# Stores of a dilated convolution: one hardware queue, or a software queue for six of eight pairs

## The chip, the cores and the metric

The kernel runs on one core of one Trainium2 chip. Its time is the device time of one execution in microseconds (us), from three runs. A profile of one further execution shows what each engine did: PE is TensorE (matmuls), DVE VectorE, ACT ScalarE, POOL GpSimd, and SP SyncE, which here only issues transfers. Sixteen DMA engines move the data between the chip's main memory and the core's on-chip memory.

## The reference

A 3x3 convolution with dilation 2 and padding 2 over 16 images of 64 channels, 64 x 64 pixels, to 128 channels, all in float32:

```python
x_pad = np.pad(x, ((0, 0), (0, 0), (pad, pad), (pad, pad)), mode='constant')   # pad = 2
for b in range(batch):            # 16
    for co in range(c_out):       # 128
        for ci in range(c_in):    # 64
            for kh in range(k):   # 3
                for kw in range(k):
                    output[b, co] += weight[co, ci, kh, kw] * x_pad[b, ci, kh*dilation:kh*dilation+h, kw*dilation:kw*dilation+w]
```

The input is 16.8 MB and the output 33.6 MB, so two thirds of the traffic are stores.

## The kernel before, in words

Two images form a pair: their 2 x 64 channels fill the 128 partitions, and there are eight pairs. A pair is loaded as one float32 tile of 2 MB (`load`, L65; pair 0 in two pieces), into a ring of three (`XF`). Each pair is worked in four groups of 16 rows, so there are 32 groups G. For a group, `cast` turns the float32 rows into float16 (L83 on ACT, L85 on POOL for four early groups), `rowsum` adds neighbouring pairs of rows on DVE (L95), and `product` runs the matmuls (L186) into three PSUM tiles: psP from the row sums, psA for the even and psB for the odd blocks of rows. ACT copies psP to `p_sb` (L248), and DVE adds it to psA and to psB (L254) and writes the finished rows to the output ring `o_ring`. That ring holds three pairs (`OB`), two images of 2 MB each: the place of pair p is written again by pair p + 3, so its stores must have ended by then.

The order of all instructions is written out by hand (a manual schedule): every engine runs its own in program order. The table `CASTS` says in which group a cast stands: from pair 3 on, a cast stands eight groups (for the last two pairs six) ahead of the group that uses it, in ACT's order just behind the copy of p_sb. A cast that waits for its load therefore holds up ACT, and with it the p_sb copies of later groups. The table `LOADS` says after which group a load is issued: pair 3 after group 0, 4 after 2, 5 after 3, 6 after 7, 7 after 11; it waits until the casts have emptied its place in the ring.

All transfers are issued by SP into its queue, in this order: weights, pairs 0 to 2, pair 3, a small store of the first four rows of the first image (`store(0, 0, 0, GR // 4)`, 128 KB), pairs 4 and 5, the two images of pair 0 (`pair_store`), those of pair 1, the load of pair 6, the stores of pair 2, the load of pair 7, and then the stores pair by pair. The flag `later` puts the stores of pairs 1 and 2 ahead of the load that stands in the same group. The last pair is stored by halves; one piece of its second image goes as 124 and 4 partitions. A store waits on SP until DVE has written its rows, and what follows it on SP waits too.

Of the kernel before, what the change touches and what calls it, by code (L numbers as in the profile page):

```python
# [10 lines left out]
def kernel(  # L11
# [7 lines left out]
    nc = tc.nc  # L19
# [16 lines left out]
    GR = 16  # L36
    NG = H // GR
    NBLK = GR // 4
    NH = GR // 2 * W
    npairs = B // 2  # L40
# [21 lines left out]
    def load(pb, cuts=(0, H)):  # L62
        x32_tiles[pb] = fpool.tile([P, HW], f32, tag="x32", name="x32")
        for lo, hi in zip(cuts[:-1], cuts[1:]):
            nc.sync.dma_start(  # L65
                out=x32_tiles[pb][:, lo * W : hi * W], in_=x_pair[pb, :, lo * W : hi * W]
            )
# [3 lines left out]
    def o_pair(pb):  # L71
        at = pb % OB * 2 * HW
        return o_ring[:, at : at + 2 * HW]
# [13 lines left out]
    def rowsum(c):  # L87
        pb, g = divmod(c, NG)
        if g == 0:
            xs_tiles[pb] = sxpool.tile([P, HW // 2], f16, tag="xs", name="xs")  # L90
        v = x16_tiles[pb][:, g * GR * W : (g + 1) * GR * W].rearrange(
            "p (b e q) -> p b e q", e=2, q=2 * W
        )
        s = xs_tiles[pb][:, g * NH : (g + 1) * NH].rearrange("p (b q) -> p b q", q=2 * W)
        nc.vector.tensor_tensor(out=s, in0=v[:, :, 0], in1=v[:, :, 1], op=add)  # L95
# [76 lines left out]
    def casts(G):  # L172
        for c, eng in CASTS.get(G, ()):
            cast(c, eng)

    def product(ps, src, kind, blk0, nblk, first, last):
        for j in (1, 0, 2):
            dw = (j - 1) * d
            o0, o1 = max(0, -dw), W - max(0, dw)
            t = kind * KW + j  # L180
            for hb in range(2):
                pp = slice(hb * CI, (hb + 1) * CI)
                rhs = src(pp, dw + o0, dw + o1)
                po = ps[:, hb * NH + blk0 * 2 * W : hb * NH + (blk0 + nblk) * 2 * W]
                po = po.rearrange("p (r w) -> p r w", w=W)[:, :, o0:o1]
                nc.tensor.matmul(  # L186
                    out=po,
                    lhsT=w_sb[pp, t * CO : (t + 1) * CO],
                    rhs=rhs,
                    start=first and j == 1,  # L190
                    stop=last and j == 2,
                )

    def blocks(x16, b0, n, e):
        v = x16.rearrange("p (b e r w) -> p b e r w", e=2, r=2, w=W)
        return lambda pp, c0, c1: v[pp, b0 : b0 + n, e, :, c0:c1]

    def store(pb, m, r0=0, r1=H, rows=((0, P),)):
        for lo, hi in rows:
            nc.sync.dma_start(  # L200
                out=out_img[2 * pb + m, lo:hi, r0 * W : r1 * W],
                in_=o_pair(pb)[lo:hi, m * HW + r0 * W : m * HW + r1 * W],
            )

    def pair_store(pb):
        for m in range(2):
            store(pb, m, GR // 4 if pb == m == 0 else 0)

    LOADS = {0: (3,), 2: (4,), 3: (5,), 7: (6,), 11: (7,)}
    FOUR = ((0, P - 4), (P - 4, P))  # L210
# [2 lines left out]
    for G in range(ngroups):  # L213
        pb, g = divmod(G, NG)
        x16 = x16_tiles[pb]
        xs = xs_tiles[pb].rearrange("p (r w) -> p r w", w=W)
        o = o_pair(pb).rearrange("p (m b e q) -> p m b e q", m=2, e=2, q=2 * W)
        b0 = g * NBLK

        def summed():  # L220
            ps = ppool.tile([P, 2 * NH], f32, tag="p", name="psP")
            sv = lambda pp, c0, c1: xs[pp, g * GR // 2 : (g + 1) * GR // 2, c0:c1]
            product(ps, sv, 0, 0, NBLK, True, True)
            return ps

        def even():
            ps = apool.tile([P, 2 * NH], f32, tag="ab", name="psA")
            product(ps, blocks(x16, b0, NBLK, 1), 1, 0, NBLK, True, False)
            z = 1 if g == 0 else 0
            product(ps, blocks(x16, b0 + z - 1, NBLK - z, 1), 2, z, NBLK - z, False, True)  # L230
            return ps

        def odd():
            ps = apool.tile([P, 2 * NH], f32, tag="ab", name="psB")
            product(ps, blocks(x16, b0, NBLK, 0), 3, 0, NBLK, True, False)
            z = 1 if g == NG - 1 else 0
            product(ps, blocks(x16, b0 + 1, NBLK - z, 0), 4, 0, NBLK - z, False, True)
            return ps

        if G == 0:  # L240
            psA, psP, psB = even(), summed(), odd()
        else:
            psP, psA, psB = summed(), even(), odd()

        if not G:
            casts(-1)
        p_sb = spool.tile([P, 2 * NH], f32, tag="psb", name="p_sb")
        nc.scalar.copy(out=p_sb, in_=psP)  # L248
        casts(G)
        if G + 1 < ngroups:  # L250
            rowsum(G + 1)
        pv = p_sb.rearrange("p (m b q) -> p m b q", m=2, q=2 * W)
        for e, ps in ((0, psA), (1, psB)):
            nc.vector.tensor_tensor(  # L254
                out=o[:, :, b0 : b0 + NBLK, e],
                in0=ps.rearrange("p (m b q) -> p m b q", m=2, q=2 * W),
                in1=pv,
                op=add,
            )

        later = pb in (1, 2)
        if g == NG - 1 and later:
            pair_store(pb)
        for q in LOADS.get(G, ()):
            load(q)
        if G == 0:
            store(0, 0, 0, GR // 4)
        if pb == npairs - 1:
            if g % 2 == 1:
                store(pb, 0, (g - 1) * GR, (g + 1) * GR)  # L270
                if g == 1:
                    store(pb, 1, 0, 2 * GR - ROWS4)
                    store(pb, 1, 2 * GR - ROWS4, 2 * GR, FOUR)
                else:
                    store(pb, 1, (g - 1) * GR, (g + 1) * GR)
        elif g == NG - 1 and not later:
            pair_store(pb)


# [33 lines left out]
```

## Time and profile before

| What | Value |
|---|---|
| Time of three runs | 126.86 us median (126.48 to 128.02) |
| Time of the profiled execution | 126.87 us |
| Its span, first to last instruction | 125.1 us |
| Busy share of PE, DVE, ACT, POOL | 84%, 72%, 49%, 5% |
| Data in SP's queue (q1) | 50.63 MB, 96.6% of the sixteen DMA engines' time |
| Read and written | 17.07 MB and 33.55 MB |
| Stores of a whole image | 13 of 2048 KB, 20.6 us (median) from issue to landing |

The page of the profile gives, for each engine, its busy time and share, then the span in 40 slices with a digit for each engine (9 is 90% busy or more), the DMA engines' busy share and the data rate in GB/s. Groups and waits are listed by source line (L254 is line 254 of the kernel). A table of stretches gives the same quantities for any times that one asks for; a list in order of time gives start, duration, engine, line, operation, and in brackets how long the engine was idle before it and what ended that wait. SPq stands for SP's issuing of transfers, not for the transfers.

### The profile page before, as it was taken

How to read it: one execution, taken by the hardware profiler on the slowest of the kernel's cores; microseconds unless marked ns; L12 is line 12 of the kernel's file. 1: busy time of each engine (PE TensorE's matmuls, PEld its weight loads, DVE VectorE, ACT ScalarE, POOL GpSimd, SP SyncE). 2: the span in 40 equal slices, each digit the busy share in tenths (PEclk: the TensorE clock that was granted, in tenths of full speed). 3: DMA queues.
4: the chain of work that ended last, by engine and by line, in shares of the span. 5: the costliest groups of instructions: out<-in, count | busy, mean ns of one | idle time of the engine just before them, and what ended most of it. 6: DMA issues, size and time to landing. Idle time of an engine off the chain costs nothing.

```text
span 125.1 us, 2341 instructions
## 1 busy us (share of the span) xinstructions
PE 105.5 (84%) x1000; PEld 56.6 (45%) x1000; DVE 90.4 (72%) x103; ACT 61.2 (49%) x64; POOL 6.1 (5%) x12
## 2 busy tenths in 40 slices
PE   6999999989999999999999999999999999300000
PEld 2355555535555555555555555555555555100000
DVE  0566969859998889888988898888988887700000
ACT  4279597396666666666336665666533333000000
POOL 2402306000000000000000000000000000000000
PEclk9999999999999999999999999999999999995555
DMA  4999999999999999999999999999999999999991
GB/s 136 376 447 440 440 419 424 419 440 419 287 419 436 424 430 440 411 424 445 424 422 430 424 419 445 430 424 424 435 430 414 435 440 424 424 419 411 430 390 63
DMA packets 4322, 50.78 MB, mean 406 GB/s; under 512 B 472, under 2 KB 600, under 8 KB 1112
## 3 DMA queue, kind: packets, MB, share of 16 engines
q1 hardware_dynamic: 4312, 50.63, 96.6%
q8 instruction: 8, 0.13, 0.4%
q14 instruction: 2, 0.02, 0.0%
HBM read 17.07 MB, written 33.55 MB: 405 GB/s over the span
## 4 chain that ended last, share of the span: by engine, by line
PE 64%; DVE 1%; DVEq 1%; issue 0%
PE psA L186 26%; PE psB L186 25%; PE psP L186 13%; DVE osb L254 1%; DVEq L308 1%; DVEq L254 0%
## 5 line engine op out<-in xcount | busy, mean ns | idle before, releaser
L186 PEld LDWEIGHTS <-w_sb 64*128 64x128 f16 x960 | 54.3, 94 | 45.6 <-issue 1.0
L248 ACT COPY p_sb<-psP 128x1024 f32<-128x1024 f32 x32 | 32.4, 1011 | 36.1 <-issue 18.6
L254 DVE TENSOR_TENSOR osb<-psA,p_sb 128x1024 f32<-128x1024 f32 x32 | 39.2, 1224 | 13.4 <-PE psA L186 7.6
L186 PE MATMUL psA<-x,w_sb 64*128 64x496 f16 (+3 forms) x384 | 45.1, 365 | 0.1
L186 PE MATMUL psB<-x,w_sb 64*128 64x496 f16 (+3 forms) x384 | 45.1, 365 | 0.0
L254 DVE TENSOR_TENSOR osb<-psB,p_sb 128x1024 f32<-128x1024 f32 x32 | 39.0, 1220 | 0.0
L83 ACT CAST x<-x 128x1024 f16<-128x1024 f32 (+2 forms) x27 | 28.2, 1051 | 4.4 <-DMA x<-in_x_dram 4.4
L186 PE MATMUL psP<-xs,w_sb 64*128 64x496 f16 (+1 forms) x192 | 26.0, 372 | 0.5 <-ACT p_sb L248 0.5
L95 DVE TENSOR_TENSOR xs<-x 128x512 f16<-128x512 f16 x32 | 13.3, 416 | 0.5 <-ACT x L83 0.5
L111 PE MATMUL dm<-zero 128*128 128x512 f16 x10 | 4.6, 580 | 1.2 <-DVE zero L103 1.2
L85 POOL CAST x<-x 128x896 f16<-128x896 f32 (+1 forms) x4 | 3.9, 987 | 12.5 <-DMA x<-in_x_dram 12.5
L111 PEld LDWEIGHTS <-zero 128*128 128x128 f16 x10 | 1.1, 124 | 2.7 <-issue 1.4
L121 DVE CAST wd<-w 128x192 f16<-128x192 f32 x1 | 0.5, 505 | 2.4 <-DMA w<-in_weight_dram 2.4
L134 PEld LDWEIGHTS <-wd 128*64 128x64 f16 x30 | 1.3, 140 | 2.1 <-DVE wd L121 1.1
L134 PE MATMUL wt<-ident,wd 128*64 128x128 f16 x30 | 1.9, 278 | 0.2 <-DVE wd L121 0.2
L123 ACT ACT_TABLE_LOAD x1 | 1.3, 1283 | 0.7 <-PEq L294 0.7
L146 ACT CAST w_sb<-wt 128x384 f16<-128x384 f32 x1 | 0.5, 478 | 2.0 <-PE wt L134 2.0
L148 DVE CAST w_sb<-wt 128x384 f16<-128x384 f32 x1 | 0.6, 558 | 1.2 <-PE wt L134 1.2
L123 ACT CAST wd<-w 128x192 f16<-128x192 f32 x1 | 0.5, 538 | 1.5 <-DMA w<-in_weight_dram 1.5
L122 POOL TENSOR_TENSOR wd<-w 128x192 f16<-128x192 f32 x1 | 0.8, 796 | 2.3 <-DMA w<-in_weight_dram 2.3
L103 DVE MEMSET zero<- 128x256 uint32 x1 | 0.3, 272 | 0.9 <-PEq L294 0.9
L125 POOL CAST wd<-w 128x192 f16<-128x192 f32 x1 | 0.8, 800 | 0.0
(12 smaller groups left out, 4.4 us busy)
## 6 DMA issues: line engine op xcount, KB each, us to landing
out_dram<-osb SPq DMA_DIRECT2D x13, 2048.0 KB, 20.6
x<-in_x_dram SPq DMA_DIRECT2D x7, 2048.0 KB, 14.8
out_dram<-osb SPq DMA_DIRECT2D x3, 1024.0 KB, 14.9
out_dram<-osb SPq DMA_DIRECT2D x1, 1920.0 KB, 19.0
x<-in_x_dram SPq DMA_DIRECT2D x1, 1088.0 KB, 5.5
x<-in_x_dram SPq DMA_DIRECT2D x1, 960.0 KB, 7.4
out_dram<-osb SPq DMA_DIRECT2D x1, 768.0 KB, 16.4
w<-in_weight_dram SPq DMA_DIRECT2D x1, 288.0 KB, 2.8
```

What stands on the lines that cost most here:

```text
L83: eng.copy(out=out, in_=in_)
L85: eng.tensor_copy(out=out, in_=in_)
L95: nc.vector.tensor_tensor(out=s, in0=v[:, :, 0], in1=v[:, :, 1], op=add)
L111: nc.tensor.matmul(out=dm[:, 0:512], lhsT=zero[:, 0:P], rhs=zero)
L122: nc.gpsimd.tensor_tensor(out=wdv[:, 3], in0=wv[:, 0], in1=wv[:, 1], op=sub)
L123: nc.scalar.copy(out=wdv[:, 2], in_=wv[:, 0])
L125: nc.gpsimd.tensor_copy(out=wdv[:, 4], in_=wv[:, 2])
L134: nc.tensor.matmul(out=wts[k % 3][r * CI : (r + 1) * CI, c0 + j * CO : c0 + (j + 1) * CO], lhsT=wd[:, t * CI : (t + 1) * CI], rhs=ident,)
L186: nc.tensor.matmul(out=po, lhsT=w_sb[pp, t * CO : (t + 1) * CO], rhs=rhs, start=first and j == 1, stop=last and j == 2,)
L248: nc.scalar.copy(out=p_sb, in_=psP)
L254: nc.vector.tensor_tensor(out=o[:, :, b0 : b0 + NBLK, e], in0=ps.rearrange("p (m b q) -> p m b q", m=2, q=2 * W), in1=pv, op=add,)
L308: with _tile.TileContext(nc) as tc:
```

## The change

The stores of pairs 0 to 5 are issued from GpSimd, through its software queue, in place of SP; those of pairs 6 and 7 stay on SP. The early store of four rows is gone, and the first image of pair 0 is stored whole. The flag `later` is gone as well: in a group with both, the load now stands ahead of the pair's stores in the program. Loads stay on SP, in the same groups. The stores on GpSimd stand in its program order behind its casts of groups 0 to 3, and it has no other work after these.

```diff
+    SOFT = range(npairs - 2)
+
     def store(pb, m, r0=0, r1=H, rows=((0, P),)):
+        queue = nc.gpsimd if pb in SOFT else nc.sync
         for lo, hi in rows:
-            nc.sync.dma_start(
+            queue.dma_start(
                 out=out_img[2 * pb + m, lo:hi, r0 * W : r1 * W],
                 in_=o_pair(pb)[lo:hi, m * HW + r0 * W : m * HW + r1 * W],
             )
 
     def pair_store(pb):
         for m in range(2):
-            store(pb, m, GR // 4 if pb == m == 0 else 0)
+            store(pb, m)
...
-        later = pb in (1, 2)
-        if g == NG - 1 and later:
-            pair_store(pb)
         for q in LOADS.get(G, ()):
             load(q)
-        if G == 0:
-            store(0, 0, 0, GR // 4)
         if pb == npairs - 1:
...
-        elif g == NG - 1 and not later:
+        elif g == NG - 1:
             pair_store(pb)
```

## The prediction

> **What bounds the kernel now.** I read the page from the top, then the stretches, then the waits of single instructions.
>
> ```profile
> PE 105.5 (84%) x1000; PEld 56.6 (45%) x1000; DVE 90.4 (72%) x103; ACT 61.2 (49%) x64; POOL 6.1 (5%) x12
> DMA  4999999999999999999999999999999999999991
> q1 hardware_dynamic: 4312, 50.63, 96.6%
> out_dram<-osb SPq DMA_DIRECT2D x13, 2048.0 KB, 20.6
> ```
>
> PE is the busiest engine, but the DMA engines are full in every slice but the first and the last, and all data goes through one queue, SP's (q1). A 2 MB store lands 20.6 us after its issue though it needs only 4.9 us: the rest is queue ahead of it.
>
> ```profile
> 30.00:33.00 3.00, 3.00 (x33) 1.69 (x30) 2.91 (x4) 1.85 (x2) 0.00 (x0) 1.00 1.00 306
> 33.00:36.00 3.00, 3.00 (x34) 1.71 (x31) 2.83 (x4) 2.06 (x2) 0.00 (x0) 1.00 0.95 389
> 36.00:60.00 24.00, 24.00 (x238) 13.17 (x234) 21.19 (x25) 14.61 (x16) 0.00 (x0) 1.00 1.01 430
> 60.00:108.00 48.00, 47.45 (x460) 25.81 (x456) 42.13 (x46) 22.73 (x23) 0.00 (x0) 1.00 1.01 428
> 108.00:120.00 12.00, 0.00 (x0) 0.00 (x0) 0.80 (x1) 0.00 (x0) 0.00 (x0) 0.67 1.00 419
> 120.00:123.00 3.00, 0.00 (x0) 0.00 (x0) 0.00 (x0) 0.00 (x0) 0.00 (x0) 0.50 0.71 298
> ```
>
> The last columns are the DMA engines' busy share and GB/s. The rate is 428 to 430 in the long stretches, also in 36 to 60 us, where loads stand among stores. It dips once, in 30 to 36 us (1.1 us lost). After 108.8 us nothing computes and some 14 us of stores are still draining. So **bytes at 428 GB/s set the end**: a 2 MB image (2.097 MB) is 4.9 us, and the change can lose time wherever DMA runs dry or slows, and gain only what DMA wastes now.
>
> ```profile
> 24.75 1.15 ACT L83 CAST x<-x 128x1152 f16<-128x1152 f32 x1 [2.19 <-DMA x<-in_x_dram]
> 34.85 1.16 ACT L83 CAST x<-x 128x1152 f16<-128x1152 f32 x1
> 59.81 1.23 DVE L254 TENSOR_TENSOR osb<-psA,p_sb 128x1024 f32<-128x1024 f32 x1 [0.15 <-ACT p_sb L248]
> 84.98 1.22 DVE L254 TENSOR_TENSOR osb<-psA,p_sb 128x1024 f32<-128x1024 f32 x1 [0.58 <-DMA out_dram<-osb]
> ...
> 22.11 13.53 SPq L200 DMA_DIRECT2D out_dram<-osb  x4
> 35.74 0.60 SPq L65 DMA_DIRECT2D x<-in_x_dram  x1
> ```
>
> These fix the order of the queue. Call the load of pair p Lp and its two stores Sp. L3 has landed at 24.7. Then come L4, L5, S0, S1, L6, S2, L7, S3: 12 images, 58.8 us, less 0.3 for the piece of S0 that went early, plus the dip: S3 lands at 84.3. The trace has DVE waiting for S3 (its place in the ring of three output pairs) until 84.98. So the hand schedule holds within 0.7 us, and I use it for the change.
>
> **The change, part by part.** The profiled execution took 126.87 us, the median of the three times is 126.86; its span is 125.1, so 1.8 us lie around the span. I sum against 126.87.
>
> *Issues.* Twelve 2 MB stores leave SP for POOL, and the 128 KB store of four rows goes into its image. SP's issues took 0.33 to 0.70 us each; POOL's store issue has no row. POOL's last other work is its casts, ending at 21.51 us, ahead of the first store in its order, so no compute queues behind a store; even 1 to 2 us each (a POOL cast is 1.0, nearest row of that engine) is 12 to 24 us on an engine that is empty for 100. From issue to first byte I take 2 us (the 288 KB weight load on SP landed in 2.8 whole); bounds 0.3 and 10, because L4 and L5 keep DMA fed to 34.5 us. Sum 0; without that backlog it is the full 2 us per store.
>
> *SP's waits.* SP no longer stands 75.6 us in L200 for DVE. L6 was issued at 35.74, behind S1; now it follows its cast (31.84 + 0.94 = 32.8), and L7 likewise 45.2 instead of 48.06. Neither load starts earlier for that, as others are ahead of it. Sum 0.
>
> *Order.* This is the main part: stores now meet loads on the DMA engines instead of standing behind them. No row shows two data queues at once. Bounds: all turns to loads gives the old order, 0; all turns to stores is the first rival, +9. I take equal turns, as both queues then hold 16 KB rows. From 24.2 us (store issue at 22.1 plus 2) each gets half: an image takes 9.8 us.
> - L4 24.7 to 34.5 us; ACT's cast wants it at 34.85. It just fits, 0 to 1 us late.
> - L5 lands at 44.3 (cast wants it at 47.2), L6 54.1, L7 63.9, both early enough.
> - S0 is out at 44 and pair 3 writes its place from 47.4: fine. S1 is out at 63.6, but DVE writes pair 4 there from 59.8: **a new stall of 3.8 us** of DVE, and of PE behind it.
> - Then S2 73.4, S3 83.2, S4 93.0, S5 102.8, alone on the engines.
>
> The stall goes into the backlog. S6 is finished at 96.4 now (end of DVE's last add of that pair), at 100.2 then, plus 1.4 to first byte: 101.6, before S5 is out at 102.8. DMA doesn't run dry, and compute ends at 112.6 with 10 us of stores queued. The reserve in all is 102.8 - 96.4 - 1.4 = **5.0 us of delay free; beyond it each us of compute costs about one.** Sum 0.
>
> The Trainium skill (DMA: Bandwidth & Descriptors, "Queues, rings and completion order") says an engine goes round-robin between its rows and drains a whole packet, typically 9 to 17 descriptors, from one before it switches. Packets of equal size on both queues would give my sum; a software packet of an image's eight rows against single rows on SP's side would give the first rival. No run here shows which.
>
> *Rate of the software stores.* 12 images are 25.2 MB, 58.8 us. No row has that queue. Bounds: the best slice (447 GB/s) gives -2.5 us, the dip's 306 gives +23.5. The nearest row, the same 16 KB rows in SP's queue, gives 0; I take 1% slower, +0.6, because the bounds are lopsided.
>
> *The dip* may not return: -1.1 to 0; I take 0. **Sum: 126.87 + 0.6 = 127.5 us.**
>
> **Rivals.**
>
> *Stores win the turns* (slower). The wait that decides is ACT's cast of L4 at 34.85: ACT is in order, so p_sb of each later group, DVE and PE stand behind it. At two store turns to one of loads L4 lands at 39.1, 4.3 us late, inside the reserve. At three to one it lands at 43.8: 8.9 late, less 5.0 is +3.9, 130.8. Stores strictly first: S0 to 34.0, then 2.6 us of L4, S1 from 36.6 to 46.4, L4 at 48.7: 13.9 late, +8.9, 135.8. I price it at 134. For it: by 24 us POOL has two whole images outstanding, and four soon after. Against: equal 16 KB rows on both sides.
>
> *The software queue moves its rows more slowly* (slower). 2% of the time is reached at 4.1% on 58.8 us; 10% is +6.5, 133.4. For it: in 120 to 123 us the share is 0.71, so the sixteen engines already don't end together, and if each has a fixed part of every image, one that lags carries its lag to the end. Against: mixing costs nothing in 36 to 60 us. The Trainium skill (same page, "Latency and other measured facts") says that DMA engines 7 and 15 are usually slower, with software-made descriptors as its best guess. It states no size; the uneven end in this trace, with no such queue, shows a lag that the guess doesn't cover.
>
> *Faster.* If the dip goes (-1.1), the uneven end closes (0.29 of 3 us, -0.9) and stores run at 440 instead of 428 (-1.6) it is 123.3; I price it at 123.8. Against: none of the three alone passes 2%, and nothing in the change touches the rate.
>
> *It changes nothing*: the engines serve SP's queue first and the order is the old one: 126.9.
>
> **Chances.** Equal turns 38% (127.5, own range 125.5 to 129.3), stores win 25% (134), slower queue 25% (133), faster 8% (123.8), no change in order 4% (126.9). Half the weight lies above the forecast's own range, because the bound on that side is wide and the reserve is 5 us. A difference of 2% (2.5 us) is about what a measurement of this kernel can tell from none: faster than 124.3: 8%; within: 42%; slower than 129.4: 50%. The range 124.5 to 136 leaves out most of the faster case and the tail of the slow ones.
>
> **What would show it.** Right: a new software queue with about 25 MB beside q1, DMA at 9 in all slices from the second on, rate near 428; SP without waits for DVE before the last pairs; landing of stores nearer 10 us early on; one DVE wait of 2 to 5 us on out_dram at pair 4, none longer; last DVE near 112 us and some 10 us of draining after it. Stores won if ACT waits for in_x_dram by more than 6 us near 35 us and DMA shows slices under 9 after 60 us. A slow queue if the slices stay at 9 with GB/s under 410. The forecast is wrong if the last DVE lies beyond 114 us, or if the loads still land before the stores.

## The result and the profile after

The changed kernel took 128.09 us (median of 20 runs, 126.89 to 128.83), the kernel before 126.72 us (median of 20); the ratio is 1.0087, with a 95% interval of 1.0059 to 1.0115. It is slower by just under one per cent, inside the 2% that were called "within". Times here are medians of all runs; the ratios leave out runs more than 1.5% above the fastest of the same kernel. The profiled execution took 127.47 us with a span of 125.7 us.

The page first: the DMA engines' busy share by slices, the two data queues (packets, MB, share of the engines' time), and the store issues on POOL.

```profile
DMA  5999999999999999999999999999999999999970
q1 hardware_dynamic: 2440, 25.46, 49.0%
q0 software_dynamic: 1728, 25.17, 47.0%
out_dram<-osb POOLq DMA_DIRECT2D x12, 2048.0 KB, 20.5
```

Half of the bytes have moved to a queue of their own, and the engines are as full as before. The median store still takes 20 us from issue to landing: the queue that it stands behind is another one, not a shorter one. The prediction's sign "nearer 10 us early on" wasn't seen: the first two stores took 16.0 and 25.5 us.

The same stretches as before (the last columns are granted clock, DMA share and GB/s):

```profile
24.00:27.00 3.00, 2.81 (x28) 1.34 (x24) 2.13 (x3) 1.70 (x2) 0.00 (x0) 1.00 1.00 344
36.00:60.00 24.00, 24.00 (x236) 13.28 (x234) 21.11 (x24) 14.91 (x16) 1.53 (x3) 1.00 1.01 430
60.00:96.00 36.00, 33.31 (x322) 15.72 (x320) 28.76 (x33) 17.92 (x19) 3.16 (x6) 1.00 1.01 428
120.00:123.00 3.00, 0.00 (x0) 0.00 (x0) 0.00 (x0) 0.00 (x0) 0.00 (x0) 0.50 0.67 281
```

430 GB/s with two queues side by side, and 428 GB/s from 60 to 96 us, where after the first few us nothing but the software queue moves data. Its rows are not slower. The dip is there again, but earlier: 24 to 27 us here, 30 to 33 us before. In both kernels it begins in the packets of a load, just ahead of the first packet of a large store (26.8 us here, 33.6 us before). PE, on the other hand, is busy 33.3 of 36 us from 60 to 96 us; before, it had no such hole.

The queues in the 30 us in which loads and stores meet (view of the DMA queues, 30 to 60 us):

```profile
q0 software_dynamic: 445, 6.50, 50.9%
q1 hardware_dynamic: 441, 6.31, 49.3%
```

These are equal turns to 3% in bytes, with rows of 16 KB on both sides. What they do to the waits is seen in the order of time (start, duration, engine, line; in brackets the idle time before and what ended it):

```profile
22.59 1.24 POOL L203 DMA_DIRECT2D out_dram<-osb  x2 [0.24 <-DVE osb L257]
35.40 1.16 ACT L83 CAST x<-x 128x1152 f16<-128x1152 f32 x1
64.83 1.23 DVE L257 TENSOR_TENSOR osb<-psA,p_sb 128x1024 f32<-128x1024 f32 x1 [4.62 <-DMA out_dram<-osb]
66.10 1.45 PE L186 MATMUL psB<-x,w_sb 64*128 64x512 f16 x12 [2.67 <-DVE osb L257]
100.05 2.37 SPq L203 DMA_DIRECT2D out_dram<-osb  x2
```

ACT's cast of pair 4 (35.40) did not wait for its load, so the loads were in time. DVE waited 4.6 us at pair 4 for the stores of pair 1, PE stood behind it, and the stores of pair 6 were issued at 100.05 us, 3.6 us later than before (96.46). The chain of work that ended last names the store that DVE waited for, issued at 35.95 us and landed 28.76 us later:

```profile
35.95 28.76 DMA out_dram<-osb
```

The same issue of pair 6's stores in the kernel before:

```profile
96.46 0.91 SPq L200 DMA_DIRECT2D out_dram<-osb  x2
```

There is a smaller wait ahead of this one, at pair 3, whose first add began at 47.44 us before:

```profile
48.94 1.23 DVE L257 TENSOR_TENSOR osb<-psA,p_sb 128x1024 f32<-128x1024 f32 x1 [1.11 <-ACT x L83]
```

The line names a cast on ACT as what ended the wait, but the second image of pair 0, which has to be out before this add writes its place, landed at 48.81 us, and the second profile of this kernel (again, below) lists two waits of DVE for stores, 6.8 us in all and 5.1 the longest, so that the other is 1.7. Pair 0's stores were late in part because the software queue's first packet moved only 4.2 us after its issue (22.59 to 26.8 us). The wait at pair 4 swallows this one: it ends when pair 1's store lands, whenever pair 3 was done.

The 20 times are not spread evenly. Eight lie between 126.89 and 127.50 (mean 127.23), twelve between 128.02 and 128.83 (mean 128.41), and none between. The profile above is of the lower group. So there were two things to explain: some 0.5 us in every run, and 1.2 us more in most.

### The profile page after: what moved, and what is told of

It is laid out like the page before. It is cut to its first block, busy times and chain, and to the rows that moved or that the text cites. A ratio compares the mean times of both kernels' runs of the same rounds, so it can differ in the third digit from the quotient of the medians.

```text
span 125.7 us, 2339 instructions
## 1 busy us (share of the span) xinstructions
PE 105.1 (84%) x1000; PEld 52.8 (42%) x1000; DVE 90.0 (72%) x103; ACT 61.2 (49%) x64; POOL 12.6 (10%) x24
## 4 chain that ended last, share of the span: by engine, by line
PE 35%; DMA 23%; DVE 8%; DVEq 1%; issue 1%; POOL 0%
DMA out_dram<-osb 23%; PE psB L186 14%; PE psA L186 14%; DVE osb L257 7%; PE psP L186 7%; DVEq L306 1%; DVE xs L95 1%; POOL out_dram L203 0%; DVEq L257 0%
## 5 line engine op out<-in xcount | busy, mean ns | idle before, releaser
L186 PEld LDWEIGHTS <-w_sb 64*128 64x128 f16 x960 | 50.8, 94 | 53.6 <-issue 4.6
L203 POOL DMA_DIRECT2D out_dram<-osb x12 | 6.5, 546 | 60.1 <-DVE osb L257 60.1
L111 PE MATMUL dm<-zero 128*128 128x512 f16 x10 | 4.1, 532 | 1.2 <-DVE zero L103 1.2
L134 PE MATMUL wt<-ident,wd 128*64 128x128 f16 x30 | 1.4, 224 | 0.2 <-DVE wd L121 0.2
L156 ACT CAST x<-x 128x512 f16<-128x512 f32 x1 | 0.6, 618 | 1.1 <-DMA x<-in_x_dram 1.1
L153 DVE CAST x<-x 128x640 f16<-128x640 f32 x1 | 0.5, 494 | 0.9 <-DMA x<-in_x_dram 0.9
```

Of the source, the lines that this page charges most:

```text
L111: nc.tensor.matmul(out=dm[:, 0:512], lhsT=zero[:, 0:P], rhs=zero)
L134: nc.tensor.matmul(out=wts[k % 3][r * CI : (r + 1) * CI, c0 + j * CO : c0 + (j + 1) * CO], lhsT=wd[:, t * CI : (t + 1) * CI], rhs=ident,)
L186: nc.tensor.matmul(out=po, lhsT=w_sb[pp, t * CO : (t + 1) * CO], rhs=rhs, start=first and j == 1, stop=last and j == 2,)
L203: queue.dma_start(out=out_img[2 * pb + m, lo:hi, r0 * W : r1 * W], in_=o_pair(pb)[lo:hi, m * HW + r0 * W : m * HW + r1 * W],)
```

## The experiments

Theory A, from the prediction: the queues take equal turns, a late store stalls DVE, the stall is free while it fits the reserve before pair 6's stores, and costs about one to one beyond it. Theory B: the software queue costs time by itself, for each image that goes through it. Theory C: the new program order costs it.

### Fewer images through the software queue, and none

Three kernels, each with another set of pairs on GpSimd. The first keeps the old order and moves pairs 3 to 5 only:

```diff
     def store(pb, m, r0=0, r1=H, rows=((0, P),)):
+        queue = nc.gpsimd if pb in (3, 4, 5) else nc.sync
...
-            nc.sync.dma_start(
+            queue.dma_start(
```

> The kernel before, with only the stores of pairs 3, 4 and 5 issued from GpSimd: the software queue without any load beside it (all loads have landed or are ahead in SP's queue), and with the old order for pairs 0 to 2. Theory A: no stall at pair 4, reserve intact, only the longer end (more completion waits on SP, some 0.3 us): ratio 1.001 to 1.004. Theory B: half of the software images, half of the cost: 1.004 to 1.006, with a rate below 425 GB/s from 70 to 100 us.

The second is the changed kernel with pairs 0 to 2 only (`SOFT = range(3)`):

> The changed kernel with only the stores of pairs 0, 1 and 2 on GpSimd; pairs 3 to 5 go back to SP. Loads and stores take turns as in the changed kernel. Theory A: the stall at pair 4 is there (4 to 5 us) and so is the whole cost: ratio 1.006 to 1.011. Theory B: half of it, 1.004 to 1.006.

The third is the changed kernel with every store on SP (`SOFT = ()`):

> The changed kernel's program order (loads ahead of stores, no early piece of four rows, whole images) with every store on SP. Theory A: one queue, so no turns; the load of pair 6 stands ahead of pair 1's stores, which land near 60.5 us, so DVE waits about 1 us at pair 4 and that is inside the reserve: ratio 0.998 to 1.003. Theory C (the new program order costs the time, not the queue): 1.006 to 1.012.

| Software images | Time (us) | Ratio to before, 95% |
|---|---|---|
| pairs 0 to 5 (the change, once more) | 128.04 | 1.0089 (1.0054 to 1.0125) |
| pairs 3 to 5 | 130.13 | 1.0266 (1.0230 to 1.0302) |
| pairs 0 to 2 | 136.63 | 1.0728 (1.0687 to 1.0769) |
| none, new program order | 126.88 | 1.0002 (0.9987 to 1.0017) |

Theory C falls: the order alone costs nothing (DVE waited 1.1 us at pair 4, as expected, and it was free). Theory B can't explain the table, since half of the images cost three and eight times as much as all of them; a small cost for each image isn't excluded by it. But my own numbers for these two kernels were far off, because I had taken the turns into account only between loads and stores. Stores in two queues take turns as well. With pairs 0 to 2 on GpSimd, the queues from 62 to 84 us, and then DVE at pair 5:

```profile
q1 hardware_dynamic: 336, 4.98, 52.9%
q0 software_dynamic: 314, 4.44, 47.4%
```

```profile
85.12 1.23 DVE L257 TENSOR_TENSOR osb<-psA,p_sb 128x1024 f32<-128x1024 f32 x1 [7.09 <-DMA out_dram<-osb]
```

Pair 3's stores, which are needed last, go out on SP's queue in every other turn, while pair 5 waits for pair 2's on the software queue. DVE stood still 15.0 us for stores in all, three times, and that is beyond any reserve: two slices of its page, from 91 to 98 us, show 107 and 0 GB/s. With pairs 3 to 5 on GpSimd it is the same the other way round: pair 3's stores take turns with pair 2's on SP (pair 3's first image landed at 75.49 us, pair 2's second at 75.45), and also with the last load.

```profile
75.58 1.23 DVE L255 TENSOR_TENSOR osb<-psA,p_sb 128x1024 f32<-128x1024 f32 x1 [3.41 <-DMA out_dram<-osb]
...
85.65 1.15 ACT L83 CAST x<-x 128x1152 f16<-128x1152 f32 x1 [5.43 <-DMA x<-in_x_dram]
```

So the full change is cheaper than either half because it keeps the stores of six pairs in one order.

### The reserve

3.8 us more of PE work at pair 5, in the kernel before and in the changed one:

```diff
-            product(ps, sv, 0, 0, NBLK, True, True)
+            for _ in range(7 if G == 20 else 1):
+                product(ps, sv, 0, 0, NBLK, True, True)
```

> The kernel before, with the psP product of group 20 (pair 5) run seven times instead of once into the same tile: 6 x 0.63 = 3.8 us more on PE, and everything behind it later by that. Theory A: the reserve before pair 6's stores is 5.0 us, so 3.8 us of late compute cost nothing: ratio 0.998 to 1.004, although DVE ends near 112.5 us. Rival: compute sets the end (PE is the busiest engine), ratio 1.03.

> The changed kernel with the same 3.8 us on PE at group 20. Theory A: its reserve is used up by the stall at pair 4 (the stores of pair 6 are issued at 100.1 us, first byte 1.4 later, and the first DMA engine is through with pair 5 at about 101.6), so nearly all of it is added: 3 to 4 us on the changed kernel, 130.5 to 132 us, ratio 1.030 to 1.042, with DMA dry between 100 and 106 us. Rival: the stall at pair 4 had not touched the reserve, ratio as without it, 1.007 to 1.012.

The kernel before took 127.12 us with it, ratio 1.0046 (1.0020 to 1.0073): of 3.8 us, 0.35 came out at the end. The changed kernel took 131.28 us, ratio 1.0342 (1.0293 to 1.0391): 3.2 us on its own 128.09. Its four times lie in two pairs, 130.5 and 132.1 us on average, 3.3 and 3.7 us above the two groups without the delay (127.23 and 128.41). The stretch from 104 to 106 us shows where, first in the kernel before with the delay:

```profile
104.00:106.00 2.00, 2.00 (x22) 1.11 (x20) 2.00 (x2) 0.27 (x1) 0.00 (x0) 1.00 1.07 459
```

and in the changed kernel with it:

```profile
104.00:106.00 2.00, 2.00 (x24) 1.19 (x22) 1.84 (x3) 1.01 (x1) 0.00 (x0) 1.00 0.19 82
```

PE is as busy in the one as in the other, and DVE nearly; the DMA engines differ, full in one and dry (19%) in the other. (The second profile, at 131.99 us, is of the upper pair, so the loss of clock of the next section is in it too.) The change has spent the reserve: what was nearly free before costs nearly in full after.

The kernel before with the delay says something else as well. It issues pair 6's stores as late as the changed kernel does without one:

```profile
100.21 0.82 SPq L200 DMA_DIRECT2D out_dram<-osb  x2
```

It does so with every transfer in SP's queue, and it too is slower, by 0.35 us. So the half microsecond in every run of the changed kernel need not come from the software queue: that compute ends so late may be enough. This was not tested further.

### The two groups of times

> The changed kernel once more, for a second profile. Its times lie in two groups, 126.9 to 127.5 and 128.0 to 128.8 us; the profile so far is of the lower group. Theory A (the reserve): equal turns make the first pairs' stores late, DVE stalls about 4.6 us at pair 4, and the stores of pair 6 then come just as pair 5's end; where they come a little later the DMA engines run dry there and the run is in the upper group. Expected ratio 1.006 to 1.012; a profile of the upper group then shows a DMA share under 1 or a low rate between 96 and 110 us. Theory B (the software queue itself): its rows or its issues cost time in every stretch; an upper profile shows a rate under 425 GB/s between 36 and 96 us.

This gave 126.87 to 128.68 us, again in both groups, and a profile at 127.59, near the lower one. One more profile fell in the upper group:

> The changed kernel once more, for a profile of the upper group of times (128.0 to 128.8 us), if it falls there. Theory A expects in it a lower DMA share between 96 and 110 us than in the profile at hand (1.01 to 1.02).

It took 128.36 us. DVE's stall is the same (4.49 us, ending at 64.63). What differs is PE behind it, in order of time and by stretches (upper group):

```profile
65.91 2.49 PE L186 MATMUL psB<-x,w_sb 64*128 64x512 f16 x12 [2.53 <-DVE osb L257]
```

```profile
66.00:70.00 4.00, 4.00 (x24) 1.81 (x25) 3.99 (x5) 0.27 (x1) 0.00 (x0) 0.57 1.00 428
...
100.00:102.00 2.00, 2.00 (x24) 1.16 (x22) 1.84 (x4) 1.01 (x1) 0.00 (x0) 1.00 0.84 352
```

The first of these stretches in the lower group's profile (after), and then in the changed kernel with the delay of the section before:

```profile
66.00:70.00 4.00, 3.87 (x36) 1.74 (x37) 4.00 (x6) 1.53 (x2) 0.00 (x0) 1.00 1.03 438
...
66.00:70.00 4.00, 4.00 (x24) 1.84 (x22) 3.87 (x5) 0.59 (x1) 0.00 (x0) 0.57 1.02 434
```

The twelve psB matmuls take 2.49 us, where the lower group's profile has 1.45. The granted clock is 0.57 from 66 to 70 us; in the lower group's it was 1.00, with 36 matmuls instead of 24. The stores of pair 6 are then issued at 101.34 us, 1.3 us later still, the DMA engines' share falls to 0.84 between 100 and 102 us, and the end moves. Pair 6's stores are now 4.9 us later than in the kernel before (96.46), and that is too much, so the reserve was less than the prediction's 5.0 us. The Trainium skill (TensorE: Matmul & The Clock Gate, "Part 1: The HAM clock gate") says that the clock goes to half after an idle window of about 3.4 us that runs freely and doesn't start with the kernel. The trace agrees on about the half and on chance in the outcome; but the idle stretch here was only 2.5 us, so by this measurement shorter gaps can do it. Nor does the length of the gap decide alone: the clock fell after 2.53 us here and in the profile with the delay, and stayed at 1.00 after 2.67 us (after), 2.75 us (after_lateloads, below) and 3.11 us (again).

The other runs have no profile, but the record has the mean granted clock over each run's span: 0.940 to 0.950 in the twelve upper runs, 0.950 to 0.964 in the eight lower ones. The clock behind the last matmul counts in this mean, so it supports the reading and doesn't prove it.

To test the clock apart from DVE's stall, PE was kept busy in those 2.5 us, with the psP product of group 17 run four times more (range 5 at `G == 17` in the same place as above):

> The changed kernel with the psP product of group 17 run five times instead of once into the same tile: 4 x 0.63 = 2.5 us more on PE, in the 2.7 us in which PE stands idle before psB of that group while DVE waits for pair 1's stores. Theory A1 (the clock): in the upper group PE's granted clock falls to about half for 3 us after that idle stretch, which puts everything behind it later by 1.2 us, more than the reserve left. With PE kept busy the clock stays up and the upper group (128.0 to 128.8 us) is gone: 126.9 to 127.6 us, ratio 1.002 to 1.006. Rival A2 (DVE's stall alone, with chance in the landings, makes the two groups): they stay, ratio 1.007 to 1.012.

127.17 us, ratio 1.0052 (1.0024 to 1.0079). Two of twelve runs are above 128.0, where the changed kernel had twelve of twenty. Once more, beside another kernel:

> The kernel with PE kept busy in the stall (group 17's psP product run five times) once more, beside the next one on the same chip: 127.0 to 127.3 us, ratio 1.002 to 1.007, with some 0.4 us of it behind the last landing.

127.34 us, ratio 1.0042 (1.0026 to 1.0059), none of eight above 128.0. DVE still waited 3.6 us for pair 1's stores, and in the stretches PE is busy 2.00 of 2.00 us with the clock at 1.00 (after_fill):

```profile
64.00:66.00 2.00, 2.00 (x22) 0.89 (x20) 1.32 (x2) 0.37 (x1) 0.00 (x0) 1.00 0.98 418
66.00:68.00 2.00, 2.00 (x22) 0.95 (x20) 2.00 (x3) 0.65 (x1) 0.00 (x0) 1.00 1.08 459
```

Pair 6's stores were issued at 100.39 and 100.55 us in the two profiles, not at 101.34. Of the changed kernel's 27 runs, 17 are above 128.0 us, with PE kept busy 2 of 20. So the upper group is the clock's, nearly all of it, with the stall as the cause: more work for PE made the kernel 0.7 to 0.9 us faster in the median.

### Taking the stall away

A first try missed. The loads of pairs 6 and 7 were put later in the program (`LOADS = {..., 12: (6,), 16: (7,)}`):

> The changed kernel with the loads of pairs 6 and 7 issued after groups 12 and 16 instead of 7 and 11, so that fewer loads take turns with the stores of pairs 0 and 1. Worked out as in the prediction: pair 1's stores land near 58 us, before pair 4 writes their place at 59.8. Theory A: no stall at pair 4, reserve back to 4 us or more, and the upper group of times (128.0 to 128.8) is gone: 127.0 to 127.4 us, ratio 1.002 to 1.005, the rest being the longer end. Rival: the upper group belongs to the software queue and not to the reserve; it stays, ratio 1.007 to 1.012.

It took 127.29 us, ratio 1.0060 (1.0033 to 1.0086), with three of nine runs above 128.0, and DVE still waited 4.7 us. The edit did not do what I meant: with the stores gone from SP's order, nothing stands ahead of these loads but the casts that they wait for, and SP had issued all of them by 45.6 us, as in the changed kernel (46.1). The place in the program no longer sets the time.

The second try puts both loads into the software queue, behind the stores of pairs 1 and 2:

```diff
-            nc.sync.dma_start(
+            (nc.gpsimd if pb in (6, 7) else nc.sync).dma_start(
                 out=x32_tiles[pb][:, lo * W : hi * W], in_=x_pair[pb, :, lo * W : hi * W]
...
+        if G < 7:
+            for q in LOADS.get(G, ()):
+                load(q)
...
         elif g == NG - 1:
             pair_store(pb)
+        if G >= 7:
+            for q in LOADS.get(G, ()):
+                load(q)
```

> The changed kernel with the loads of pairs 6 and 7 issued from GpSimd too, behind the stores of pairs 1 and 2 in its order, so that in the software queue they can't take turns with these stores. Only the loads of pairs 4 and 5 still meet stores. Theory A: pair 1's stores land by about 55 to 57 us, the stall at pair 4 is gone, the reserve is back and the upper group of times as well: 126.9 to 127.5 us, ratio 1.002 to 1.005, the rest being the longer end. Rival (the software queue costs by itself): ratio 1.007 to 1.012 as before.

126.83 us, ratio 1.0003 (0.9987 to 1.0018), all twelve runs between 126.53 and 127.39. Pair 4's first add, in order of time:

```profile
59.87 1.22 DVE L257 TENSOR_TENSOR osb<-psA,p_sb 128x1024 f32<-128x1024 f32 x1 [0.15 <-ACT p_sb L251]
```

No wait for a store, and the whole cost of the change is gone, though the software queue now carries 29.36 MB, more than in the changed kernel. This is the plainest evidence against theory B. It equals the kernel before, and no version here was faster than that one.

### The last half microsecond

With the clock kept up, 0.4% stays. Besides the late end of compute (see the reserve), the traces show one more candidate. In the trace of the changed kernel, 1.26 us lie between the last landing and the end of the span; before it was 0.89. SP waits there for eight completion counts of each queue in a fixed order, 0.06 us apart. In the changed kernel six such waits follow the landing that comes last; in the kernel before it was one, and in the one with the loads behind the stores none. The next kernel keeps PE busy as above and moves that landing to the end of the order by splitting loads:

```diff
-    load(2)
+    load(2, (0, H // 2, H))
...
-            load(q)
+            load(q, (0, H // 2, H))
```

> The same kernel with the loads of pairs 2 to 7 issued in two halves each, so that SP issues 24 transfers and not 18. Completions are counted on eight semaphores for SP's queue in turn; at the end SP waits for each of them in a fixed order, 0.06 us apart, and in the changed kernel the transfer that lands last counts on an early one, so six waits follow its landing. With 24 the last to land is on the last. Theory E (the end waits make 0.4 us): 126.6 to 126.9 us, ratio 0.999 to 1.002. Rival (the 0.4 us are something else of the software queue): 127.0 to 127.3, ratio as that of the kernel beside it.

127.38 us, ratio 1.0046 (1.0028 to 1.0064), as the kernel beside it (1.0042). The stretch behind the last landing was 0.89 us again, but the time didn't follow. Splitting twelve megabytes of loads may have cost what the end gained; this is not shown.

The split did more than move a landing. A half image has rows of 8 KB, and the queues from 30 to 60 us (fill_split) were

```profile
q0 software_dynamic: 584, 8.52, 66.6%
q1 hardware_dynamic: 583, 4.25, 33.7%
```

Packets are equal in number (a data packet of the profile is one row here), bytes two to one: the queues take turns row by row, and the queue with rows half as long gets a third of the rate. The stores gained by it. The second image of pair 1 landed at 58.73 us, not 64.70, DVE waited for no store at pair 4 (its 2.95 us there were for the extra products), and pair 6's stores were issued at 98.27 us. So this kernel has neither the stall nor the longer end, and still the 0.4%, while the kernel with every store on SP issued them at 98.30 us and cost nothing. Where these 0.4% arise stays open.

## Why the prediction was right, and where it was not

- **What bounds the kernel**: bytes at 428 GB/s. It held in every run with full DMA slices.
- **Order**, the main part: equal turns, taken between two bounds, were what the queues did (6.50 and 6.31 MB), and for the reason given, equal rows: with rows of 8 KB against 16 the bytes were one to two. The Trainium skill's round-robin (DMA: Bandwidth & Descriptors, "Queues, rings and completion order") agrees with the trace; turns of whole packets on one side alone would not have given equal bytes. Pair 4's load was in time, as worked out; the stall of DVE at pair 4, 3.8 us in the sum, was 4.6; pair 6's stores, expected at 100.2, came at 100.05. The stall went into the backlog, as said: DMA was full in the lower group. One step failed without harm: pair 0's stores were to be out at 44 us, "fine" for pair 3, and landed at 48.81, so that DVE waited there too.
- **The reserve of 5.0 us**: the idea was right, the size too large. In the lower group pair 6's stores came 3.6 us later than before and DMA stayed full; in the upper profile they came 4.9 us later, which 5.0 would have covered, and DMA ran dry. So it lies between these two, and the delay of 3.8 us, almost free before and 3.2 us after, fits that. The sum let all sixteen engines end pair 5 together at 102.8 us; that some are through earlier may be the difference, which is not shown.
- **Issues**: POOL's took 546 ns on average where 1 to 2 us were allowed, and hid, as expected. The time to the first byte was mis-sized: 2 us were taken, and the first software packet came 4.2 us after its issue (4.9 in again); the loads kept DMA fed meanwhile, as the sum said, and it showed only in pair 0's late landing. The 1.4 us to the first byte of pair 6's stores had no row; the traces have 0.9 to 1.2. The longer end was not in the sum at all.
- **Rate of the software stores**, +0.6 us: the term is mis-sized. It measured zero (428 GB/s), and the kernel with 29.36 MB through that queue costs nothing. The lopsided bounds were no reason to leave the nearest row.
- **"Sum 0" for the stall** failed in one step. I said that PE stands behind DVE and stopped there. What an idle PE can lose next is its clock: 1.2 us in most runs, which went past the reserve that there was, though not past the 5.0 us of the sum. This and the unexplained 0.4% make the 1.4 us between the medians, where the sum had 0.6 for another reason. The total came out close, partly by luck.
- **The rivals**: stores did not win the turns, since ACT did not wait for pair 4's load. (Its two mixed cases don't add up: two and three store turns to one of loads give 39.4 and 44.3 us from 24.7, not 39.1 and 43.8; nothing hangs on it.) The queue was not slower; the lag of single engines that the Trainium skill (DMA: Bandwidth & Descriptors, "Latency and other measured facts") ties to software-made descriptors shows in no rate here. The faster case fell because the dip came back and the end stayed uneven (0.67 in 120 to 123 us). The order was not the old one. The first rival's mechanism, something needed late because another queue takes turns, did decide two of the experiments, with stores against stores.

## What to carry to other kernels

A second queue added no bandwidth here, where the DMA engines were full; it changed the order from first come to equal turns. So list what is needed soonest on each queue and, with rows of equal size, halve its rate wherever the other queue holds work. Keep transfers with due times in one queue, in the order of these times, and give the second only what can wait or what must not stand behind a wait. When a stall looks free, follow it through every engine behind it, PE's clock included, and subtract it from a reserve that you have worked out.

## What was not expected of the hardware

- PE's granted clock fell to 0.57 for some 4 us after 2.53 us without matmuls (again2, after_delay), and not after 2.67, 2.75 and 3.11 us (after, after_lateloads, again).
- Two queues shared the DMA engines by packets of the profile (rows), not by bytes: 584 and 583 packets, 8.52 and 4.25 MB, where one had rows of 16 KB and the other of 8 KB (fill_split).
- The rate dips for some 3 us, from just ahead of the first packets of the large stores, whichever queue these are in (306 GB/s in 30 to 33 us before, 344 in 24 to 27 us after); why was not tested.
- SP's issue of two stores took 2.37 us in the changed kernel (at 100.05 us) and 0.91 us before (at 96.46 us), though both went to the same hardware queue. In the lower group it was hidden by the backlog; with the delay, when DMA was dry, the two took 0.96 us (at 105.10).
